# Ordering a two-block transformer program by a time-line simulation

## The chip, the core and the metric

The kernel runs on one core of a Trainium2 chip, in one launch. The metric is the device time of that core in microseconds (us). Its engines are TensorE (PE, with its weight loads as PEld), VectorE (DVE), ScalarE (ACT), GpSimd (POOL) and SyncE (SP), whose queue issues nearly all DMA transfers here. Each engine runs its own list of instructions in order and waits on semaphores for the others.

## What is computed

One sequence of 512 tokens of width 1024, in fp32, passes through three layers. The first is an RWKV-7 time mix with a squared-ReLU MLP. The second shares keys and values, runs a forgetting attention and a second MLP. The third adds two branches, a gated delta rule that runs forwards and backwards and a latent attention (MLA), and then an expert-choice mixture of 16 experts. The reference, cut to its frame:

```
def reference(x, c, ...):
    x = first_block(x, c, ...)      # for i in range(2): mix (rwkv7 | forgetting attention), then MLP
    return second_block(x, c_2, ...)

# second_block
h = rms_norm_2(x, g_mix) * (1.0 + sc1) + sh1
proj = h @ w_in
y_dn = gated_deltanet_branch(dn_qkv, dn_z, dn_b, dn_a, ...) @ w_o_dn
y_mla = mla_branch(c_q, c_kv, k_r, ...) @ w_o_mla
x = x + gt1 * ((g_dn * y_dn + g_mla * y_mla) @ w_out)
h = rms_norm_2(x, g_ffn) * (1.0 + sc2) + sh2
x = x + gt2 * expert_choice_ffn(h, w_router, w_gate, w_up, w_down)
return rms_norm_2(x, g_final)
```

Each of the three layers is modulated by shifts, scales and gates, which are products of a vector c with matrices of 1024 x 6144.

## The kernel before

Activations lie feature-major in SBUF, as eight tiles of 128 x 512 (128 features, 512 tokens). A dense product splits both operands into a high half in fp32r and a low half, and adds three products (lines 244 to 246 in dense_cols; 272 to 274 in dense_tmc; line 1323 in dense_gen). The split of weights is in wsplit: SP loads a raw tile (line 179), ACT copies it into the high half (line 181), and DVE or POOL subtracts to get the low half (line 183). Raw, high and low tiles have two buffers each. The split of activations is the same in two steps (lines 201 and 202).

The program is traced in one go and in the order of the layers, and the order of each engine's instructions is set afterwards, when the TileContext is left. The scheduler then runs a simulation of the chip; on each engine it issues, among the instructions whose inputs are ready at that simulated moment, the one with the best priority. The priority is the place in the trace, and "behind(by)" moves what is traced inside it back by so many places, so that it fills gaps. "issue_after(ins)" and "keep_in_program_order" add edges: what they cover is queued on its engine behind a given instruction, without a wait. Slots of a pool are given out in the same simulation. The order that comes out is fixed: at run time every engine takes its list as it stands.

The stages, with their times in the profiled execution: vectors of modulation and the dense products of the time mix (0 to 225 us), pairs and scan of the time mix (225 to 600), the first MLP (600 to 900), the forgetting attention (900 to 1275), the second MLP (1275 to 1575), the mixer with the delta rule (1575 to 2250), the rest of the latent attention and the output products (to 2470), the route and the 16 experts (to the end).

In the MLPs the modulation of the later layers is computed by DVE as a filler (mod_vgen, lines 376 and 378). In the mixer the delta rule's two head groups (dn_group) have normal priority, and the latent attention with the remaining input products (mla_gen, by way of dense_gen) is traced under behind(), a million places back, as the filler:

```
with self.behind():
    self.run(self.mla_gen(cks, H, ym))
self.run(self.dn_group(bp, lambda: tA, 0, gs, Zs, yd))
self.run(self.dn_group(bp, lambda: [self.fetch(t) for t in tB], 1, gs, Zs, yd))
```

Each group inverts 32 triangular blocks at once on DVE (tri_inverse2): 62 steps, each a multiply and an add (lines 1400 and 1402, then 1407 and 1409), then eight transposes (lines 1413 and 1414), behind which PE's small products start (line 1422). In the latent attention DVE multiplies by a gain and a norm (line 1812), and the result is split by lines 201 and 202.

The experts' weights come through a ring of 16 tiles of 1 MB (load, line 2081); the first five are queued between the loads of w_out by edges. Two experts share PE, 64 rows each (lines 2134 and 2162).

## Time and profile before

| what | value |
|---|---|
| median of 3 runs | 2994.79 us (2993.59 to 2998.83) |
| the profiled execution, its own time | 2999.24 us |
| its span, first to last instruction | 2997.4 us |
| PE busy, share of the span | 2766.3 us, 92% |
| DVE, ACT, POOL busy | 54%, 35%, 24% |
| mean granted clock of PE | 0.954 |

A page of the profile gives busy times by engine, a course in 40 slices and the costliest groups of instructions. The trace behind it is asked for tables by stretch of time, for who waited for whom, for the chain of work that ended last, and for the instructions of an engine in order of time. A wait is counted where an engine sat idle ahead of an instruction, and is put down to what ended it.

### The profile page before, as it was taken

How to read it: one execution, taken by the hardware profiler on the slowest of the kernel's cores; microseconds unless marked ns; L12 is line 12 of the kernel's file. 1: busy time of each engine (PE TensorE's matmuls, PEld its weight loads, DVE VectorE, ACT ScalarE, POOL GpSimd, SP SyncE). 2: the span in 40 equal slices, each digit the busy share in tenths (PEclk: the TensorE clock that was granted, in tenths of full speed). 3: DMA queues.
4: the chain of work that ended last, by engine and by line, in shares of the span. 5: the costliest groups of instructions: out<-in, count | busy, mean ns of one | idle time of the engine just before them, and what ended most of it. 6: DMA issues, size and time to landing. Idle time of an engine off the chain costs nothing. (4 is left out here: it accounts for less than half of the span.)

```text
span 2997.4 us, 38061 instructions
## 1 busy us (share of the span) xinstructions
PE 2766.3 (92%) x15046; PEld 1971.0 (66%) x15046; DVE 1615.5 (54%) x2449; ACT 1049.1 (35%) x1703; POOL 726.7 (24%) x563
## 2 busy tenths in 40 slices
PE   6998888999999999999999997998799997999997
PEld 1765666788876777788886775766677874444333
DVE  4568745465673367566636789638755442111112
ACT  2555523422234466422223542353344322110001
POOL 2456633211110043111113353144141121000000
PEclk9998777999999999999999999999999998999999
DMA  6324215355672321465432223142252359999998
GB/s 214 120 85 151 77 58 176 99 175 190 196 242 66 101 61 50 133 205 182 156 97 84 80 81 113 51 134 74 61 179 85 106 192 355 350 389 409 409 409 304
DMA packets 361010, 502.05 MB, mean 167 GB/s; under 512 B 24768, under 2 KB 236992, under 8 KB 360832
## 3 DMA queue, kind: packets, MB, share of 16 engines
q1 hardware_dynamic: 349600, 479.01, 47.0%
q10 hardware_dynamic: 11232, 20.62, 1.9%
q8 instruction: 118, 1.93, 0.3%
q14 instruction: 60, 0.49, 0.0%
HBM read 471.26 MB, written 26.21 MB: 166 GB/s over the span
## 5 line engine op out<-in xcount | busy, mean ns | idle before, releaser
L244 PE MATMUL psb<-s,wh 128*128 128x512 f32 x1384 | 542.8, 392 | 2.7 <-DVE s L988 1.9
L245 PE MATMUL psb<-s,wl 128*128 128x512 f32 x1384 | 540.4, 390 | 0.0
L246 PE MATMUL psb<-s,wh 128*128 128x512 f32 (+1 forms) x1320 | 514.7, 390 | 1.5 <-POOL s L481 0.6
L181 ACT ACTIVATE wh<-wr 128x1024 fp32r<-128x1024 f32 (+1 forms) x221 | 288.1, 1304 | 397.9 <-PE psb L246 263.9
L183 DVE TENSOR_TENSOR wl<-wr,wh 128x1024 fp32r<-128x1024 f32 (+1 forms) x145 | 260.7, 1799 | 262.8 <-ACT wh L181 260.4
L244 PEld LDWEIGHTS psb<-s,wh 128*128 128x128 f32 x1384 | 259.4, 187 | 70.7 <-issue 11.4
L245 PEld LDWEIGHTS psb<-s,wl 128*128 128x128 f32 x1384 | 259.5, 188 | 56.5 <-issue 2.2
L246 PEld LDWEIGHTS psb<-s,wh 128*128 128x128 f32 (+1 forms) x1320 | 247.4, 187 | 58.5 <-issue 2.9
L183 POOL TENSOR_TENSOR wl<-wr,wh 128x1024 fp32r<-128x1024 f32 (+1 forms) x76 | 185.5, 2443 | 401.4 <-ACT wh L181 386.1
L2134 PE MATMUL psb<-rg,s 128*64 128x512 f32 x1024 | 242.9, 597 | 5.7 <-DMA rg<-in_w_up_dram 4.4
L1323 PE MATMUL psf<-f,wh 128*128 128x512 f32 (+1 forms) x688 | 232.3, 412 | 10.7 <-ACT wh L181 10.7
L1019 POOL TENSOR_TENSOR s<-s 128x512 f32<-128x512 f32 x64 | 102.2, 1596 | 514.8 <-ACT s L1017 434.1
L2134 PEld LDWEIGHTS psb<-rg,s 128*64 128x64 f32 x1024 | 83.1, 136 | 142.6 <-issue 120.4
L1323 PEld LDWEIGHTS psf<-f,wh 128*128 128x128 f32 (+1 forms) x688 | 133.3, 195 | 42.5 <-ACT wh L181 11.6
L1323 PE MATMUL psf<-f,wl 128*128 128x512 f32 (+1 forms) x344 | 142.7, 415 | 16.6 <-POOL wl L183 16.5
L2162 PE MATMUL psb<-rg,s 128*64 128x512 f32 (+1 forms) x544 | 129.5, 620 | 0.0
L378 DVE SCALAR_TENSOR_TENSOR mt<-mr,crep,mt 128x512 f32<-128x512 f32 x168 | 126.4, 753 | 3.6
L201 ACT ACTIVATE s<-s 128x512 fp32r<-128x512 f32 x112 | 69.8, 625 | 136.2 <-POOL s L1019 73.1
L1026 DVE SCALAR_TENSOR_TENSOR s<-psb,aff,s 128x512 f32<-128x512 f32 x64 | 45.9, 751 | 129.1 <-PE psb L246 129.1
L1323 PE MATMUL psb<-f,wh 128*128 128x512 f32 (+1 forms) x336 | 106.5, 397 | 7.8 <-DVE f L479 5.9
L1017 ACT ACTIVATE s<-psb 128x512 f32<-128x512 f32 x64 | 37.6, 588 | 164.0 <-PE psb L246 164.0
L2162 PEld LDWEIGHTS psb<-rg,s 128*64 128x64 f32 x544 | 46.2, 147 | 73.9 <-issue 69.8
(565 smaller groups left out, 4926.4 us busy)
## 6 DMA issues: line engine op xcount, KB each, us to landing
rg<-in_w_gate_dram SPq DMA_DIRECT2D x64, 1024.0 KB
rg<-in_w_up_dram SPq DMA_DIRECT2D x64, 1024.0 KB
rg<-in_w_down_dram SPq DMA_DIRECT2D x64, 1024.0 KB
mr<-in_mod_w_dram SPq DMA_DIRECT2D x96, 512.0 KB
wr<-in_mlp_down_dram SPq DMA_DIRECT2D x32, 1024.0 KB
wr<-in_mlp_up_dram SPq DMA_DIRECT2D x31, 1024.0 KB
wr<-in_w_in_dram SPq DMA_DIRECT2D x54, 512.0 KB
mr<-in_w_mod_dram SPq DMA_DIRECT2D x40, 512.0 KB
```

Source lines behind the costliest of these rows:

```text
L181: nc.scalar.activation(hi, raw, AF.Copy)
L183: (lo_eng or self.lo_eng or nc.vector).tensor_tensor(lo, raw, hi.bitcast(F32), op=OP.subtract)
L201: nc.scalar.activation(hi, src, AF.Copy)
L244: nc.tensor.matmul(pt[:mw], hi[k][:, j:j + mw], a, start=(k == 0), stop=False)
L245: nc.tensor.matmul(pt[:mw], lo[k][:, j:j + mw], a, start=False, stop=False)
L246: nc.tensor.matmul(pt[:mw], hi[k][:, j:j + mw], b, start=False, stop=(k == nk - 1))
L378: nc.vector.scalar_tensor_tensor(acc[:, hb], raw[:, d], c, acc[:, hb], op0=OP.mult, op1=OP.add)
L1019: nc.gpsimd.tensor_tensor(sq, r, r, op=OP.mult)
L1026: nc.vector.scalar_tensor_tensor(xT[m], pt, gt[:, m:m + 1], xT[m], op0=OP.mult, op1=OP.add)
L1323: nc.tensor.matmul(pt[:rows, :cols], x, y, start=(k == 0 and q == 0), stop=(k == nk - 1 and q == 2))
L2134: nc.tensor.matmul(B[n][q], XE[hp][k0 // 2][:, o:o + 64], w[e][:, k, n * 512:n * 512 + 512], start=(k0 + k == 0), stop=(k0 + k == 7), skip ...
L2162: last = nc.tensor.matmul(pt[q, :n], HT[(k + i) // 4][:, o:o + 64], w[e][i], start=(k + i == 0), stop=(k + i == 7), skip_group_check=True)
```

## The change

The context that traces and orders the program is opened with one more argument. By it the scheduler picks instructions along another simulation: one that plays the time line of each engine with its sequencer and its queues, and of the DMA queues, in place of the coarser simulation that is the default. The traced program, its priorities, edges, pools and tiles are the same.

```
--- before.py
+++ after.py
@@ -2426,7 +2426,7 @@
         A[n] = nc.dram_tensor(nm, a.shape, mybir.dt.from_np(a.dtype), kind="ExternalInput").ap()
         feed[nm] = a
     out = nc.dram_tensor("out_0_dram", (D, T), F32, kind="ExternalOutput").ap()
-    with _tile.TileContext(nc) as tc:
+    with _tile.TileContext(nc, schedule_with_timeline_sim=True) as tc:
         K(tc, nc, A, coff, poff).program(out)
     nc.finalize()
     r = _run(nc, [feed], core_ids=[0])
```

## Rows read from the trace of the kernel before

**Rows 1.** The page's first part: busy us, share of the span and count by engine.

```profile
PE 2766.3 (92%) x15046; PEld 1971.0 (66%) x15046; DVE 1615.5 (54%) x2449; ACT 1049.1 (35%) x1703; POOL 726.7 (24%) x563
```

**Rows 2.** Busy us by stage; last three columns: granted clock, DMA share, GB/s.

```profile
225.00:600.00 375.00, 325.51 (x2858) 242.09 (x2855) 242.16 (x322) 159.33 (x265) 165.64 (x193) 0.82 0.34 112
600.00:900.00 300.00, 297.49 (x1340) 241.29 (x1339) 191.46 (x221) 83.62 (x85) 41.03 (x26) 1.00 0.62 201
900.00:1275.00 375.00, 364.92 (x1781) 273.58 (x1781) 196.13 (x431) 203.33 (x376) 87.36 (x56) 1.00 0.28 82
1275.00:1575.00 300.00, 300.00 (x1341) 244.53 (x1340) 167.25 (x174) 85.26 (x88) 48.72 (x31) 1.00 0.49 159
1575.00:2250.00 675.00, 589.89 (x3667) 467.15 (x3665) 475.84 (x787) 266.21 (x477) 242.43 (x130) 0.95 0.32 95
2250.00:2425.00 175.00, 173.59 (x911) 137.28 (x910) 94.08 (x157) 69.77 (x134) 34.22 (x26) 1.00 0.32 103
2700.00:2997.00 297.00, 269.88 (x1170) 114.27 (x1166) 55.60 (x91) 28.62 (x47) 0.00 (x0) 0.97 0.97 383
```

**Rows 3.** The chain that ended last (start, us, what); one slice of the tail.

```profile
2811.20 20.40 DMA rg<-in_w_up_dram
...
2775.00:2850.00 75.00, 70.55 (x314) 29.92 (x312) 10.45 (x17) 5.83 (x10) 0.00 (x0) 0.98 1.03 409
```

**Rows 4.** Waits of PE in the whole span: us in total, times, longest us.

```profile
PE psb L1422 <- DVE T L1413: 27.2, 6, 13.2
...
PE psf L1323 <- POOL wl L183: 16.5, 11, 2.1
...
PE psf L1323 <- ACT wh L181: 10.7, 1, 10.7
PE psb L828 <- ACT W L824: 9.8, 5, 6.8
```

**Rows 5.** PE in order of time at the two inverses; in brackets the idle time before.

```profile
1877.43 0.28 PE L1422 MATMUL psb<-T,UB 32*32 32x32 f32 x2 [10.26 <-DVE T L1413]
...
2117.72 0.28 PE L1422 MATMUL psb<-T,UB 32*32 32x32 f32 x2 [13.18 <-DVE T L1413]
...
2118.53 0.63 PE L1323 MATMUL psf<-f,wl 128*128 128x512 f32 x1
...
2119.81 0.63 PE L1323 MATMUL psf<-f,wl 128*128 128x512 f32 x1
```

**Rows 6.** DVE and POOL in order of time in the two inverses.

```profile
1787.43 1.79 DVE L1400 TENSOR_TENSOR tm<-P,R 128x135 f32<-128x135 f32 x1
...
1872.00 2.28 DVE L1409 TENSOR_TENSOR R<-R,tm 128x87 f32<-128x87 f32 x1
...
2047.24 2.31 DVE L1402 TENSOR_TENSOR R<-R,tm 128x60 f32<-128x60 f32 x1
...
2055.45 2.55 POOL L183 TENSOR_TENSOR wl<-wr,wh 128x1024 fp32r<-128x1024 f32 x1 [5.99 <-ACT wh L181]
...
2055.78 2.47 DVE L1402 TENSOR_TENSOR R<-R,tm 128x231 f32<-128x231 f32 x1
2058.29 0.41 DVE L1400 TENSOR_TENSOR tm<-P,R 128x240 f32<-128x240 f32 x1
...
2102.22 2.57 DVE L1407 TENSOR_TENSOR tm<-P,R 128x255 f32<-128x255 f32 x1
```

**Rows 7.** ACT and DVE in order of time around 2066 us.

```profile
2066.66 0.63 ACT L201 ACTIVATE g<-f 128x512 fp32r<-128x512 f32 x1 [10.77 <-DVE f L1812]
...
2073.16 1.04 ACT L181 ACTIVATE wh<-wr 128x1024 fp32r<-128x1024 f32 x1
...
2065.89 0.74 DVE L1812 SCALAR_TENSOR_TENSOR f<-f,P,f 128x512 f32<-128x512 f32 x1
```

**Rows 8.** A group of instructions by line: busy us, mean ns, idle before.

```profile
L183 POOL TENSOR_TENSOR wl<-wr,wh 128x1024 fp32r<-128x1024 f32 (+1 forms) x76 | 185.5, 2443 | 401.4 <-ACT wh L181 386.1 <-PE psb L281 7.4 <-PE psf L1323 5.6
```

**Rows 9.** Waits of SP's queue of DMA issues: us in total, times, longest.

```profile
SPq L179 <- POOL wl L183: 572.6, 74, 29.1
```

More of the change, by code (lines that the diff above doesn't have):

```diff
@@ L2428 @@
     out = nc.dram_tensor("out_0_dram", (D, T), F32, kind="ExternalOutput").ap()
-    with _tile.TileContext(nc) as tc:
+    with _tile.TileContext(nc, schedule_with_timeline_sim=True) as tc:
         K(tc, nc, A, coff, poff).program(out)
```

## The prediction

> **What bounds the kernel now.** I read the page's first line, then the table by stage, then the waits of TensorE, then the time lines around its longest waits. TensorE (PE) is busy for 2766.3 of 2997.4 us, so it has 231 us of idle time in all [rows 1]. The table by stage says where that is [rows 2]. In three stretches that hold 775 us (600 to 900, 1275 to 1575, 2250 to 2425) PE is busy for 297.49, 300.00 and 173.59 us: 3.9 us of idle time at the full clock. There the order can lose time, but it has almost none to win. In the last stretch the DMA share is 0.97, and the chain of waits goes through transfers of the expert weights of 20.4 us at a time [rows 2, 3]: what orders the engines changes nothing there, except by when the ring of weights starts to fill. Two stretches are left in which order matters both ways: the scan of the first block (225 to 600, 49.5 us of idle time at a clock of 0.82) and the delta rule with latent attention as its filler (1575 to 2250, 675 - 589.89 = 85.1 us of idle time at 0.95) [rows 2].
>
> In the second of these the waits have names. PE waits 27.2 us for DVE's transposes of the triangular inverse, 16.5 us for POOL's low halves of filler weights and 10.7 us for ACT's high half of one [rows 4]. The two longest waits at the inverse are 13.18 and 10.26 us, and what PE runs right behind each are filler matmuls (line 1323) [rows 5]: PE works in order, and the order has the inverse's first two matmuls ahead of filler.
>
> **The change part by part.** No instruction is added to the trace and none is taken out, beyond the waits and table loads that follow from the order. What changes is the clock by which the scheduler picks: on each engine it takes the ready instruction of the best priority at a simulated moment. Priorities (the arguments of "behind"), the edges of issue_after and keep_in_program_order, slots and banks stay. So every wait is kept or moved by which of two ready instructions goes first, on PE, DVE, ACT and POOL and on SP's queue of DMA issues alike.
>
> First, are today's waits errors of the old order's clock? For the inverse I compared its steps. A step of 128x231 takes 2.47 us and the next, of 240, takes 0.41; the long one starts at 2055.78, while POOL's split of 1024 columns runs from 2055.45 for 2.55 us [rows 6]. Such long steps stand 13 times in the first group's inverse (from 1787.43 to 1872.00) and 8 times in the second's (2047.24 to 2102.22) [rows 6], each 1.1 to 2.3 us over its neighbours; at 2 us in the mean that is 26 and 16 us, against waits of PE of 10.3 and 13.2 us. So the stretching alone is more than the wait. An order that prices every instruction by itself keeps these 23.4 us; one that prices the collision, or that had DVE too short before, wins them. I take 0, the first of the two, as the rows explain the wait without an error of price; the end for the range is -23.4 us.
>
> The Trainium skill, "SBUF — State Buffer", section "Who interferes with whom", says that a DVE instruction with two SBUF inputs and a GpSimd instruction that reads SBUF exclude each other for the whole instruction. The trace agrees (2.47 against 0.41 us), and by this rule no price of single instructions tells when the inverse ends.
>
> The wait of 10.7 us is another kind. ACT stands for 10.77 us at a split (line 201) for a multiply of DVE (line 1812), and the high half of filler weights (line 181), which PE needs, is queued behind it at 2073.16; DVE runs these multiplies one by one between steps of the inverse [rows 7]. That is an order on ACT that took DVE's multiply for earlier than it came. Better times of DVE turn it: -10.7 us, bounds 0 and -10.7. I take all of it. The 16.5 us for POOL are the filler's own supply (2443 ns a split [rows 8]); with the inverse unfinished PE has nothing else, so 0 here, -16.5 at best.
>
> What does a new order cost where PE is full? The trace has no other order, so I bound it. The nearest rows are stretches in which the same dense code runs beside chains: 900 to 1275 has 10.1 us of idle time in 375 (2.7%), 1575 to 2250 has 85.1 in 675 (12.6%) [rows 2]. At 2.7% the 775 full us lose 20.9, or 17 more than now; at 12.6% they lose 98, or 94 more; where the new order agrees with the old, nothing. I take 17, as dense stretches with double-buffered weights are nearer to attention than to the inverse; ends 0 and 94. Behind a long wait three matmuls take 1.28 us (2118.53 to 2119.81 [rows 5]), 427 ns each, where 1341 of them fill 300 us at the full granted clock, 224 ns each [rows 2]: the lower of PE's two levels against the upper; some eight run so before the clock is back, 1.6 us for each such wait. For three new ones I add 5 us.
>
> In the two stretches with chains every pick is a new draw. Of the 85.1 us, 27.2 + 16.5 + 10.7 = 54.4 are named above, which leaves 30.7 us; of the scan's 49.5 us the largest group is 9.8 us in five waits, the longest of them 6.8 us [rows 2, 4]. These are hand-offs in small pieces, which an order from other times would undo as well as mend. I take a seventh of the 80 us as lost, 12 us, since chains that lie well can move only one way; ends -24 and +40 (30% won, half lost).
>
> SP's queue of issues is the fifth list that is ordered anew. It stands 572.6 us before weight loads (line 179) until POOL has freed a buffer [rows 9], so it runs as far ahead as the buffers let it. An issue that goes ahead of another one costs if the passed one is the next that is needed, and all loads queued behind it wait too; I take 0, with the longest single wait of this group, 29.1 us, as the end.
>
> The tail is the experts. The first loads of their ring go out between the loads of w_out, by explicit edges, and those edges stay, so 0; if the first five loads came after all of them, five loads of 1 MB at 409 GB/s [rows 3] would be 13 us, one for one at the end.
>
> Sum against the profiled execution of 2999.24 us: -10.7 + 17 + 5 + 12 = +23, so 3022.5. That execution stood 4.4 us above the median of 2994.79, so the forecast is 3018 us.
>
> **The rivals.** *The new times are the better ones, and the order wins.* For it: the 10.77 us on ACT are a mistake of timing, and the inverse has a stall in both groups. Against it: the stalls are explained by the collisions, and 775 us are full. It gives the 10.7, the 9.8, half of the 23.4 and of the 16.5 us, and a quarter of the other 70 us: 58 us, with 5 us of clock 63, less 22 us for waits and clock in the full stretches: 41 us, so some 2954 us. It decides if the new clock has DVE and POOL within some per cent of the trace (0.41 and 2.4 us); ends 2915 and 2989. Chance 0.38.
>
> *More collisions.* POOL's splits come earlier or later and meet more two-input steps of DVE. Each costs 2.06 us; less than a third of POOL's 76 splits of weights [rows 8] lie in the inverses. If 30 more meet a DVE chain that sets the pace, 62 us on DVE, of which PE cannot fill half: 31 us beside the 23 of the forecast, some 3050 us; it decides from about ten new meetings on. Chance 0.10.
>
> *The order hardly moves,* because edges and program order fix it, or the flag changes only times and no pick: 2989 to 3001 us, within 0.2%, about what a measurement of this kernel can tell from no change. Against it: the fillers are placed by readiness alone. Chance 0.12.
>
> **How the numbers follow.** Forecast (slower by new waits in full stretches and chains): 3018 us, 0.40, its own range 3001 to 3090. The collisions add 0.10 on the same side. Faster by over 0.2% 0.38, within 0.2% 0.12, slower by over 0.2% 0.50. The range of 8 in 10 goes from 2940, which leaves out the far end of the faster case, to 3090, near the bound of 94 us.
>
> **What would show it.** Right: in the table by stage PE falls under 297 of 300 us in 600 to 900 or 1275 to 1575, with new waits of PE for a low or high half of weights (lines 181 and 183); the waits of line 1422 for line 1413 stay above 15 us; the last stretch keeps its DMA share and its length from the first expert matmul to the end. The ACT wait for line 1812 should be gone. Wrong: the inverse's wait vanishes and the filler runs ahead of it (the first rival), or the idle time by stage is as it was and the difference lies in the tail, by a ring that starts to fill sooner or later. A kernel above 3100 us would mean that a queue was ordered badly as a whole, for example SP's issues, which I have priced at 29.1 and 13 us at most.

## The result and the profile after

The new order takes 3068.85 us (median of 4 runs, 3060.34 to 3070.32), the old one beside it 2996.20 us (4 runs): a ratio of 1.0239, 95% interval 1.0224 to 1.0254, so 72.7 us slower. The forecast was 3018 us, in a range of 2940 to 3090. The direction and the range held; the size did not, and the place of the loss was another one.

The page's first line answers [rows 1]. The work is the same, and PE is busy 27.4 us longer for the same 15046 matmuls (2793.7 against 2766.3), in a span that is 71.1 us longer:

```profile
span 3068.5 us, 38050 instructions
...
PE 2793.7 (91%) x15046; PEld 2000.8 (65%) x15046; DVE 1600.0 (52%) x2449; ACT 1051.6 (34%) x1706; POOL 733.3 (24%) x563
```

Next the table by stretch of time, with the columns of [rows 2], in the new kernel: the scan, a stretch of each MLP, the tail, and one slice of the tail.

```profile
225.00:600.00 375.00, 328.75 (x2877) 247.42 (x2876) 253.52 (x332) 163.44 (x273) 176.33 (x202) 0.82 0.34 111
600.00:900.00 300.00, 300.00 (x1358) 244.46 (x1357) 195.37 (x226) 84.25 (x86) 43.64 (x27) 1.00 0.63 203
1350.00:1650.00 300.00, 300.00 (x1347) 245.58 (x1346) 163.87 (x170) 82.90 (x83) 43.03 (x27) 1.00 0.47 148
2770.00:3068.00 298.00, 269.63 (x1170) 114.23 (x1166) 55.48 (x91) 28.63 (x47) 0.00 (x0) 0.98 0.98 383
2850.00:2925.00 75.00, 70.51 (x307) 29.64 (x305) 10.45 (x17) 5.83 (x10) 0.00 (x0) 0.98 1.03 409
```

The MLPs are as full as before (300.00 of 300, against 297.49 and 300.00), the scan is nearly as it was (328.75 against 325.51 us busy, clock 0.82 in both), and the tail has its 409 GB/s and its length. So the time must be lost between. Fixed stretches of time compare different work once a kernel is late, so the next table cuts both traces at the same instruction: the last update of the first MLP and that of the second (line 1026), and w_out's last matmul (line 246). First the two stretches of the kernel before, then those of the new one.

```profile
904.80:1613.40 708.60, 698.51 (x3269) 545.96 (x3268) 380.65 (x622) 297.69 (x473) 142.45 (x91) 1.00 0.37 113
...
1613.40:2469.05 855.65, 768.75 (x4599) 608.43 (x4597) 567.82 (x942) 339.10 (x616) 275.63 (x156) 0.96 0.35 105
```

```profile
906.90:1663.40 756.50, 722.67 (x3269) 562.54 (x3268) 379.40 (x622) 296.87 (x473) 148.62 (x91) 0.97 0.35 106
...
1663.40:2538.20 874.80, 768.78 (x4604) 618.01 (x4602) 547.84 (x943) 342.31 (x618) 272.92 (x156) 0.93 0.34 103
```

This is the account of the loss. The attention with the second MLP takes 47.9 us more (756.50 - 708.60): 24.2 us because the same 3269 matmuls are busy longer (722.67 - 698.51, at a lower clock), and 23.7 us of idle time (33.83 - 10.09). The mixer and the output products take 19.2 us more (874.80 - 855.65), all of it idle time, as PE's busy time is the same to 0.03 us. What lies ahead of 904.80 adds 2.1 us, what lies behind 2469.05 adds 1.9 (530.3 - 528.4). The sum is 71.1 us, the difference of the spans.

The waits of PE in the whole span, with the columns of [rows 4]:

```profile
PE psb L1422 <- DVE T L1413: 55.1, 6, 28.3
...
PE psb L828 <- ACT W L824: 13.0, 3, 7.0
...
PE psb L1224 <- DVE s L1221: 8.7, 8, 3.2
PE psb L1194 <- ACT qk L1172: 8.6, 6, 3.9
...
PE psf L1890 <- ACT f L1898: 6.6, 1, 6.6
PE psb L1657 <- POOL s L1651: 6.5, 1, 6.5
```

In the mixer the waits for weight halves are nearly gone: from 1600 to 2480 the matmuls of line 1323 that write tile psf wait 2.4 us for POOL and 0.2 for ACT, against 16.5 and 10.7 in [rows 4] (those that write psb wait 4.4 us for halves, 3.0 more than before). But the inverses' wait has doubled, from 27.2 to 55.1 us. In the attention there are more and longer waits, of 1 to 4 us (lines 1224 and 1194). Slices of the attention in the new kernel show what goes with them:

```profile
1050.00:1075.00 25.00, 25.00 (x99) 16.96 (x98) 1.23 (x1) 8.00 (x12) 5.58 (x3) 1.00 0.29 84
1075.00:1100.00 25.00, 17.07 (x74) 13.41 (x73) 13.84 (x36) 15.96 (x32) 14.40 (x9) 0.86 0.25 66
...
1125.00:1150.00 25.00, 22.37 (x101) 16.78 (x100) 12.33 (x39) 12.11 (x29) 7.76 (x5) 0.77 0.10 26
```

From 1125 to 1150 PE is busy for 22.37 of 25 us, but the granted clock is 0.77. In the old kernel these slices hold 24.3 to 24.6 us of work at 1.00.

The share of busy time hides how the clock fell, because matmuls at the lower clock are themselves busy for longer. Here is the same stretch, cut where the clock changes (columns of [rows 2]), and the waits of PE ahead of the fall (columns of [rows 5]):

```profile
1119.00:1123.70 4.70, 1.69 (x11) 1.25 (x12) 3.34 (x7) 4.58 (x13) 4.35 (x4) 0.92 0.41 99
1123.70:1133.20 9.50, 9.47 (x33) 6.84 (x34) 4.93 (x21) 2.95 (x9) 0.00 (x0) 0.50 0.13 38
1133.20:1142.00 8.80, 8.26 (x42) 6.12 (x41) 3.04 (x8) 2.04 (x5) 0.89 (x1) 1.00 0.01 2
...
1119.99 0.38 PE L1194 MATMUL psb<-qk,qk 68*128 68x256 f32 x1 [1.07 <-ACT qk L1172]
1121.43 1.31 PE L1224 MATMUL psb<-s,V 128*64 128x128 f32 x10 [1.06 <-ACT s L1219]
1123.73 0.45 PE L1216 MATMUL psb<-C,s 128*128 128x128 f32 x1 [0.99 <-DVE st L1202]
```

PE first stands idle for 3.0 of 4.7 us, in three waits of about 1 us, two of them for ACT. Behind them it runs the small matmuls of the chain for 9.5 us almost without a gap, but at 0.50, the lower of its two levels. It is back at 1.00 when the next block of filler runs.

What stands behind it is seen on ACT, in order of time, where a pair of heads begins: first the new kernel, then the old. Lines 1171 to 1173 are the copies that prepare q and k of a head, line 1201 is the exponential of a unit (its sums of 0.19 us are left out), line 1219 copies transposed scores.

```profile
1116.71 0.61 ACT L1171 ACTIVATE qk<-s 64x512 fp32r<-64x512 f32 x1
1117.35 0.63 ACT L1173 ACTIVATE qk<-s 64x512 fp32r<-64x512 f32 x1
1118.00 0.63 ACT L1171 ACTIVATE qk<-s 64x512 fp32r<-64x512 f32 x1
1118.65 0.63 ACT L1173 ACTIVATE qk<-s 64x512 fp32r<-64x512 f32 x1
1119.31 1.28 ACT L1172 ACTIVATE qk<-s 64x512 fp32r<-64x512 f32 x2
1120.61 0.40 ACT L1201 ACTIVATE s<-s,st 128x128 f32<-128x128 f32 x1
```

```profile
1112.55 0.63 ACT L1172 ACTIVATE qk<-s 64x512 fp32r<-64x512 f32 x1
1113.09 0.39 ACT L1201 ACTIVATE s<-s,st 128x128 f32<-128x128 f32 x1
...
1113.59 0.63 ACT L1171 ACTIVATE qk<-s 64x512 fp32r<-64x512 f32 x1
1114.17 0.39 ACT L1219 ACTIVATE s<-psb 128x256 f32<-128x256 f32 x1
1114.58 0.51 ACT L1201 ACTIVATE s<-s,st 128x256 f32<-128x256 f32 x1
...
1115.21 0.63 ACT L1172 ACTIVATE qk<-s 64x512 fp32r<-64x512 f32 x1
1115.86 0.62 ACT L1201 ACTIVATE s<-s,st 128x384 f32<-128x384 f32 x1
```

The new list runs the copies of both heads of a pair as one block of 3.9 us (1116.71 to 1120.6) ahead of four exponentials, and does so in each of the eight pairs. In the old list the second head's copies stand one by one between exponentials. The two waits of PE for ACT shown above fall into this block and just behind it. PE's new list fits this: the scores of the next three units stand with their second matmuls put off, transposes stand right ahead of the products that need their copies, and the gate's filler comes in blocks of 19 and 7 per eight units. That is read from the two lists of instructions; what each costs, the experiments tell as far as they can.

### The profile page after: what moved, and what is told of

Read it like the earlier page. It is cut to its first block, busy times and chain, and to the rows that moved or that the text cites. A ratio compares the mean times of both kernels' runs of the same rounds, so it can differ in the third digit from the quotient of the medians.

```text
span 3068.5 us, 38050 instructions
## 1 busy us (share of the span) xinstructions
PE 2793.7 (91%) x15046; PEld 2000.8 (65%) x15046; DVE 1600.0 (52%) x2449; ACT 1051.6 (34%) x1706; POOL 733.3 (24%) x563
## 4 chain that ended last, share of the span: by engine, by line
PE 76%; DVE 12%; DMA 7%; ACT 3%; issue 2%; POOL 0%; SPq 0%; DVEq 0%; ACTq 0%; POOLq 0%
PE psb L244 11%; PE psb L246 11%; PE psb L245 11%; PE psf L1323 6%; PE psb L2134 6%; PE psb L1323 4%; PE psb L2162 3%; DMA rg<-in_w_down_dram 2%; PE psb L1224 2%; DMA rg<-in_w_gate_dram 1%; DMA rg<-in_w_up_dram 1%; PE psm L342 1%; PE psb L273 1%; PE psb L274 1%; PE psb L272 1%
## 5 line engine op out<-in xcount | busy, mean ns | idle before, releaser
L1323 PE MATMUL psf<-f,wh 128*128 128x512 f32 (+1 forms) x688 | 222.5, 400 | 0.2 <-ACT wh L181 0.2
```

The lines of the kernel that those rows point to most:

```text
L1323: nc.tensor.matmul(pt[:rows, :cols], x, y, start=(k == 0 and q == 0), stop=(k == nk - 1 and q == 2))
```

## The experiments

Most of them hold lists. All instructions have the same names in both kernels, so a list of one order can be put on the other kernel by edges without waits. In these kernels lines of the code stand 2 further down (line 1224 is 1226), with edges in the mixer up to 9 further.

```
+def _order(tc, nc):
+    ins = {i.name: i for i in nc.cur_bb.bb.instructions}
+    for part in zlib.decompress(base64.b85decode(_LISTS)).decode().split(";"):
+        names = [f"I-{n}" for n in itertools.accumulate(int(d) for d in part.split(":")[1].split(","))]
+        for a, b in zip(names, names[1:]):
+            tc.add_manual_dep(ins[b], a, mybir.DependencyInfo(mybir.DependencyClass.NoSync, mybir.DependencyReason.DATA), reason="order")
...
         K(tc, nc, A, coff, poff).program(out)
+        _order(tc, nc)
```

**Which stage loses.** The kernel before, with the new order of all five engines in one part alone.

> The kernel before, with the new order of all five engines for the instructions of the forgetting attention alone. By the landmarks of the two traces the last update of the first MLP (line 1026) comes 2.1 us later (904.8 to 906.9) and that of the second 50.0 us later (1613.4 to 1663.4), so if each stage's loss is its own this kernel is 48 us slower than before, with a granted clock near 0.8 to 0.95 between 1075 and 1250. If the loss comes of the prediction's full stretches or of the mixer, or if it needs the new order of the stages around it, it is within 10 us of before.

> The kernel before, with the new order for the mixer and its output products alone (from the projections of the delta rule to w_out). By the landmarks the shift grows from 50.0 us to 69.2 us there (last matmul of w_out 2469.05 to 2538.2), so +19 us if stages add up: PE loses the waits for the halves of filler weights (16.5 and 10.7 us), and waits some 28 us more at line 1422. If the mixer's loss in the new kernel is only that of a stage that starts 50 us later against transfers, it is within 5 us of before.

> The kernel before, with the new order for the time mix alone. Landmarks: the first square of the first MLP (line 1019) moves from 557.2 to 563.4, so +6 us if it stays; the prediction had put half of its loss of 12 us in scan and mixer here. If the first MLP makes it up (its last update moves by 2.1 us only), +2.

> The kernel before, with the new order for the two MLPs and for the route and the experts. The prediction's step of new idle time in full stretches would give +17 to +22 us. By the landmarks: -4 us in the first MLP (its start is late by 6.2 us, its end by 2.1), +1.5 in the route and experts, so between -4 and +2.

| new order in | us | before, same chip | difference, us | ratio, 95% |
|---|---|---|---|---|
| attention | 3052.48 | 2996.05 | +56.4 | 1.0172 to 1.0203 |
| mixer, output products | 3010.23 | 2996.05 | +14.2 | 1.0036 to 1.0061 |
| time mix | 2995.23 | 2996.05 | -0.8 | 0.9992 to 1.0010 |
| MLPs, route, experts | 2992.98 | 2996.05 | -3.1 | 0.9977 to 0.9995 |

The parts add up to 66.7 of the 72.7 us. The attention holds three quarters of the loss, the mixer most of the rest; the MLPs lose nothing, against the 17 to 22 us of the forecast.

**The attention put back.** The new kernel, with the old lists of the attention.

> The new kernel with the old order of all five engines in the forgetting attention alone. If the stages are independent, the 56 us come back: 3068.9 - 56 = 3013 us, 14 to 18 us slower than before, which is the mixer. If the new order elsewhere needs the new attention, less comes back.

3021.22 against 2998.32 us before on that chip (ratio 1.0075, 1.0059 to 1.0091): 22.9 us are left of 72.7, so 50 came back. That is 5 to 9 us less than expected, near what the landmarks gave (47.9).

**PE's list or ACT's.** In the attention of the kernel before: PE's new list beside the four old ones; and ACT's new list with the other four chosen around it by the old scheduler.

> The kernel before; in the forgetting attention PE's list is that of the new kernel, the lists of ACT, DVE, POOL and SP are its own. If the loss of 56 us lies in PE's order (gate matmuls taken in one block of 19 to 24 ahead of the chain, scores pulled ahead of transposes), this kernel is 40 to 56 us slower than before. If it lies in ACT's order (the six copies of two heads in one block ahead of the exponentials), PE's order alone costs under 20 us.

> The kernel before; in the forgetting attention ACT's list is that of the new kernel (six copies of lines 1171 to 1173 in one block before the exponentials of line 1201), the other four lists are chosen anew around it by the old scheduler. If ACT's block is the cause: 30 to 56 us slower than before, as each block holds the exponentials up for 3.9 us in each of eight pairs of heads, with the clock behind it. If PE's order is the cause: under 15 us.

PE's list alone: 3039.01 against 2995.02 us, +44.0 (ratio 1.0135 to 1.0165). ACT's: 3068.48, +73.5 (1.0231 to 1.0262), more than all five new lists together. Both theories claimed 30 to 56 us for themselves and under 20 for the other, so neither expectation came true. PE's list does most of the damage by itself, and the other four new lists together add 12.4 us to it (56.4 - 44.0). The second kernel is no price of ACT's list alone, as there the old scheduler also changed the other four lists; it shows that this scheduler, held to ACT's block, finds an order worse than the new one. The waits of PE in the attention of that kernel show how ACT's block reaches PE (line 1226 is the product with V, line 1221 ACT's copy of transposed scores, which stands behind the block):

```profile
PE psb L1226 <- ACT s L1221: 31.2, 7, 5.7
PE psb L1226 <- DVE s L1223: 5.7, 2, 3.5
PE psb L1196 <- ACT qk L1174: 4.3, 1, 4.3
```

**The block broken in two,** in the new kernel.

```
-            nc.scalar.activation(a[lo], tq[q], AF.Copy)
-            nc.scalar.activation(c[lo], tk[q], AF.Copy)
-            nc.scalar.activation(b[up], tq[q], AF.Copy)
+            with tc.issue_after(self.last_act()) if hd else contextlib.nullcontext():
+                nc.scalar.activation(a[lo], tq[q], AF.Copy)
+                nc.scalar.activation(c[lo], tk[q], AF.Copy)
+                nc.scalar.activation(b[up], tq[q], AF.Copy)
```

> The new kernel with one edge: the three ACT copies of the odd head are queued behind the last ACT instruction traced before them, so that the block of six falls apart into two blocks of three. If ACT's block is the cause, 30 us or more of the 56 come back (about 3035 us or less). If PE's order is the cause, it stays within 15 us of the new kernel (3055 to 3075 us).

3056.65 us, ratio 1.0203 (1.0186 to 1.0220) against 1.0239 of the new kernel: 11 us came back. Two blocks of three copies cost less than one of six, but far from all is ACT's: the 11 us are near the 12.4 us that the lists besides PE's add.

**PE's list taken apart.** The old kernel with a PE list made of both: the chain in the new order with the gate's 206 filler matmuls at their old places, and the reverse.

> The kernel before; in the forgetting attention only PE's list is changed, and in it only the order of the chain (scores, transposes, products with V) is the new one, with the 206 gate matmuls left at their old places between the units. PE's whole new list cost 44 us. If the chain's order is the cause (in each eight units the second score matmuls of three units stand together behind products, and transposes stand right ahead of the products that need their copies), 30 to 44 us slower than before. If the filler's place is the cause, under 12.

> The counterpart: PE's chain in its old order, the 206 gate matmuls at their new places (blocks of 19 and 7 per eight units, none in the second half). If the filler taken ahead in blocks is the cause, 30 to 44 us slower than before; if the chain's order is, under 12.

The chain's order costs 16.2 us (3014.52 against 2998.32), the filler's places 22.8 us (3021.10); together 39.0 of the 44.0. Here too both expectations wanted one cause, and there are two of like size. The stretch 1069 to 1260 (columns of [rows 2]) tells them apart: new chain, new filler, PE's whole new list, all five new lists.

```profile
1069.00:1260.00 191.00, 182.08 (x984) 137.11 (x984) 118.69 (x344) 116.61 (x255) 61.20 (x41) 1.00 0.27 78
```

```profile
1069.00:1260.00 191.00, 170.63 (x913) 130.15 (x912) 117.42 (x339) 110.30 (x249) 56.88 (x39) 0.95 0.25 74
```

```profile
1069.00:1260.00 191.00, 166.61 (x883) 125.78 (x882) 111.51 (x331) 104.90 (x239) 56.05 (x39) 0.95 0.21 60
```

```profile
1069.00:1260.00 191.00, 162.79 (x805) 122.68 (x804) 103.35 (x325) 101.34 (x235) 57.16 (x37) 0.86 0.19 52
```

With filler between the units the clock stays at 1.00 even if the chain is badly ordered (182.08 of 191 us busy; the kernel before has 183.51 there). With filler in blocks, half of the units run with nothing between them, PE waits for DVE's copies (12.3 us in ten waits at line 1226), and the clock is 0.95; with the other four lists, ACT's block among them, it is 0.86.

**Filler held back in the mixer.** In the old order 447 of 1584 filler matmuls (line 1323) stand ahead of the last matmul before the first inverse and 1084 before the second; in the new one 758 and all 1584, and the latent attention too. Two edges on PE hold filler until the chain's matmul.

```
+        held = [self.fill_mm[k] for k in (447, 1084)]
...
+        for ins, last in zip(held, self.inv_after):
+            self.tc.add_manual_dep(ins, last.name, mybir.DependencyInfo(mybir.DependencyClass.NoSync, mybir.DependencyReason.DATA), reason="issue_after")
```

> The new kernel with two edges on PE in the mixer: filler matmul 447 of 1584 is queued behind the last matmul ahead of the first inverse, and filler matmul 1084 behind the last one ahead of the second, as many as the old order had put there (the new one has 758 and all 1584). If the mixer loses because the filler is used up before the second group's chain, the 14 us come back and the waits saved for halves of weights stay saved: 14 to 40 us faster than the new kernel (3028 to 3055 us), with the wait of 28 us at line 1422 under 15. If the filler's place is not the cause, within 5 us of it.

3079.34 us, ratio 1.0280 (1.0265 to 1.0295): 12 us slower than the new kernel. The count was off: 312 of the 1584 matmuls are traced earlier and are not in this list, so the edges stood at 759 and 1396, and the first held nothing. The next kernel has them at 135 and 772, on top of the old attention.

> The same with two edges on PE in the mixer, at other places than in the kernel with the two edges above, where the first edge changed nothing: filler matmul 135 of mla_gen's 1272 behind the last matmul ahead of the first inverse and number 772 behind the last one ahead of the second, so that the filler stands 519 and 1156 matmuls far at these points (old order 447 and 1084, new order 758 and 1584). If the filler that overtakes the chain is the mixer's cause, 14 us or more come back, to 3000 us or less; with the waits for weight halves saved as well, some 2985. If it is not, it is within 5 us of the kernel without the edges, or slower.

3034.42 us, 13 us slower than without the edges (3021.22). Filler held back in this way gives nothing back. The inverses' wait went down from 55.1 to 11.3 us, as the theory said, but the idle time came up elsewhere: waits of PE from 1600 to 2450, where line 1553 is the chain ahead of the inverse and lines 1325, 1405 and 1788 are lines 1323, 1400 and 1779 of the kernel before.

```profile
PE psb L1553 <- ACT s L1550: 14.3, 16, 1.2
PE psf L1325 <- DVE f L1788: 13.7, 1, 13.7
PE psf L1325 <- DVE tm L1405: 12.4, 1, 12.4
PE psb L1427 <- DVE T L1418: 11.3, 6, 3.8
```

The 12.4 us stand at the first edge (before 1808.17), the 13.7 us inside the second inverse (before 2168.94), where the filler that is next needs DVE. Cut at the inverses, PE's idle time from the last update of the second MLP to w_out's last matmul is 104.7 us with the edges and 104.8 without them. Behind the second inverse it went from 33.3 to 7.1 us, ahead of the two inverses from 27.9 to 64.0. The 12.3 us that this stretch became longer are busy time (783.6 against 771.2 us for 4608 matmuls each): the clock from the first inverse to the second is 0.88, without the edges 0.95.

**Filler put where the wait is.** The kernel before, with the first matmuls behind the inverses queued behind more filler: 46 and 107, or 46 and 54.

```
+        self.inv_fill = [self.fill_mm[k] for k in (527, 1107)]
...
+        filled = self.inv_fill.pop(0)
...
+                self.tc.add_manual_dep(i1.ins, filled.name, mybir.DependencyInfo(mybir.DependencyClass.NoSync, mybir.DependencyReason.DATA), reason="issue_after")
```

> The kernel before with two edges on PE: the first matmuls behind the inverses (line 1422) are queued behind filler matmul 527 and 1107 of mla_gen's 1272, that is 46 and 107 more filler matmuls than in the old order, 10 and 24 us of work at 224 ns each, in the waits of 10.3 and 13.2 us and the one of 10.7 us for ACT. If PE's filler sets the mixer's time, 15 to 30 us faster than before (2965 to 2980 us). If the chain's own length sets it, or the filler's weights don't come faster (POOL's halves), within 5 us, and the waits at line 1323 grow by what those at line 1422 lose.

> The same with 54 instead of 107 more filler matmuls ahead of the second inverse's first matmul (12 us for its wait of 13.2 us alone). If filler sets the time: 10 to 22 us faster than before; more than with 107 only if those overshoot the inverse's end and hold the chain up.

3004.98 us with 107 (ratio 1.0027, 1.0018 to 1.0037) and 3001.09 with 54 (1.0013, 1.0004 to 1.0022), against 2997.09: slower, where filler as the limit wanted 10 to 30 us faster. The waits of PE with 107, in the whole span, name a reason:

```profile
PE psf L1323 <- DVE f L1785: 27.0, 1, 27.0
...
PE psf L1323 <- POOL wl L183: 19.1, 12, 2.2
...
PE psb L1425 <- DVE T L1416: 8.7, 3, 3.5
```

The wait did not go, it changed its name: the filler that is next needs a multiply of the rotary embedding on DVE (line 1779 of the kernel before, 1785 here). DVE comes to it at 2138.51, behind the last steps of the inverse, its eight transposes (2117.08 to 2131.97) and the tables of the embedding; the chain's first matmul, held behind this filler, starts at 2150.85. So 107 are too many, and the filler that is next in the list is not free of DVE; whether later filler could go ahead of it was not tried. With 54 the waits at line 1425 are 28.4 us in seven pieces, no less than the 27.2 us before: in the old order PE ran nine or ten filler matmuls in each gap between the transposes, and the edges took these out, so that behind a first wait of 9.8 us three more of 3.4 us each stand open. These two kernels move cover more than they add it.

**A kernel that beats both.** The first of these with the new order of the parts that were not slower, and these parts alone.

> The first of these two with the new order of the time mix, both MLPs, route and experts, which alone were 1 and 3 us faster than before. If the parts add up, 4 us faster than the kernel with the two edges alone.

> The kernel before with the new order for the time mix, both MLPs, route and experts; attention, mixer and output products keep the old one. If the parts are independent, -0.8 and -3.1 us add up to 4 us faster than before (about 2993 us). If the time mix's gain is noise, 3 us; if the new order only helps beside the new attention, no difference.

3001.22 us, 3.8 faster than without these parts, but still behind the old kernel (1.0007 to 1.0025); and 2996.69 against 2997.40 alone (0.9986 to 1.0005), no difference. The MLPs, route and experts had shown -3.1 us by themselves; the time mix with them shows -0.7. No kernel here beats the old one by more than these 3 us, which did not come again.

## Why the prediction was right and wrong

**The step that failed is the first one of the sum: which stretches count.** The prediction split the span in full ones (775 us), the tail, and "two stretches in which order matters both ways". The attention, 900 to 1275, was in none of them. It came in only as a yardstick for others, with its 10.1 us of idle time in 375 [rows 2], and had no term of its own. It is the third chain: 64 units, each through PE, DVE, ACT and PE again, with a filler of 206 matmuls. That it was 97% full did not mean that order matters little there, but that its order was good; it lost 56.4 us by the run that changed it alone, 47.9 by the landmarks (with the MLP behind it), and 50 came back when its old order was restored. With the forecast's own way of pricing it could have had 10.1 us at the full clock turned into the mixer's 12.6% of idle time: 375 x 0.126 = 47 us, less 10, is 37. The bound was in the rows.

**New waits in the full stretches, +17, and their clock, +5: not there.** 300.00 of 300 us in both MLPs, and -3.1 us in the run. The granted clock there is 1.00, as before. Why the dense code keeps its pace under either scheduler was not tried. The yardstick was the wrong way round: what was lost, the attention lost.

**Scan and mixer, +12, and the wait for ACT, -10.7: together +1.3, measured 13.4** (-0.8 and +14.2 us). That the 12 alone is near is luck: the scan lost nothing, and the mixer's waits did not add up as the sum had them. The wait for ACT went as forecast (0.2 us now), and so did 14.1 of the 16.5 us for POOL that the forecast had put at 0. But in the mixer and the output products the idle time grew by 19.1 us all the same. Cut at the inverses (from the first step to the first matmul of line 1422), PE is idle for 49.5 us beside the two inverses before and 43.7 now; ahead of them it is 24.5 and 28.0. What is lost lies behind the second inverse, 12.9 us before and 34.3 now, in a shorter stretch:

```profile
2117.70:2469.05 351.35, 338.46 (x2136) 270.74 (x2136) 192.55 (x304) 138.22 (x260) 85.11 (x56) 0.99 0.40 127
...
2312.60:2538.20 225.60, 191.30 (x1318) 160.35 (x1318) 109.26 (x158) 62.34 (x109) 24.84 (x20) 0.89 0.39 130
```

The first line is the kernel before, which still has filler to run there; the second is the new one, in which the last of the 1584 filler matmuls ran at 2156, 89 us ahead of the second inverse.

**The inverses' wait, 0: the price was wrong, and so was its reason.** The prediction put the wait down to DVE steps that POOL stretches. In the second inverse of the new order (2245.66 to 2310.36) one of the 124 steps is stretched, to 1.41 us, and the others are not, as POOL has almost nothing left to do there; and PE waits longer than ever. These are that inverse's steps of the forms of [rows 6], and PE behind it, in order of time:

```profile
2258.64 1.41 DVE L1402 TENSOR_TENSOR R<-R,tm 128x231 f32<-128x231 f32 x1
2261.25 0.39 DVE L1400 TENSOR_TENSOR tm<-P,R 128x240 f32<-128x240 f32 x1
...
2312.64 0.31 PE L1422 MATMUL psb<-T,UB 32*32 32x32 f32 x2 [28.27 <-DVE T L1413]
```

The Trainium skill, "SBUF — State Buffer", section "Who interferes with whom", says that such a DVE instruction and a GpSimd instruction exclude each other; this trace agrees (POOL is busy 2.83 of the 50 us from 2250, and the one step of 1.41 us stands beside POOL's split of 1.29 us from 2258.51), but the wait does not follow from it. The wait of 28.3 us follows from what PE has beside the second inverse: nothing, as the filler was used up (1584 of 1584 matmuls ahead of the second group's first). Of the 27.9 us by which the waits at line 1422 grew, 15.1 are this, 3.7 the wait behind the first inverse (10.26 to 13.99, with filler left), and the rest mostly three waits of 3.4 us between the transposes of the second. In every order tried PE waits for DVE somewhere: filled with more filler the wait turns into one of 27.0 us for DVE, held back it moves ahead of the inverses and into the second. So the mixer's 14 us are idle time that the new order gathers behind the second inverse; by which few picks, no run here settles, and the cause of these 14 us stays open.

**The queue of SP, 0 with an end of 29.1.** SP stands 123.8 us once, at a fetch (line 1266) into a slot that the second group's chain frees late (line 1582). It was a wait beyond the bound; what it costs by itself was not tried, so this term stays open. **The tail, 0:** 1.9 us, right.

**The rivals.** "More collisions" is refuted: 11 long steps in the first inverse and one in the second, against 13 and 8 [rows 6], and yet slower. "Hardly moves" too. "The order wins" was right on two of the four waits that it named, those for weight halves (10.7 and 16.5 us); the wait of 9.8 us at line 828 is now 13.0, and the inverses' has doubled. It was wrong that the first two are worth anything at the end: 24.6 us of them went, and the mixer became slower.

## What to carry to other kernels

The stretch that was full beside a chain of small steps is the one that the new order spoilt most here: price such a stretch by what a like chain loses where it lies badly, not by the idle time that it has. When a scheduler is exchanged, hold the lists stage by stage and engine by engine: the loss then has an address, and a wait that vanishes can be told from a wait that only moved. A filler has an order of its own to keep: in the orders tried here more of it at a wait gained nothing, because it came out of another gap or needed the engine that the chain was waiting for.

## What the hardware showed that was not expected

A busy share of nine tenths can hide a stall and what it costs. The slice of 22.37 of 25 us at 0.77 (1125 to 1150) looks like a PE that is throttled while it works. Cut finer, the fall stands behind 4.7 us of which PE was busy for 1.69, and the lower level then held for 9.5 us in which PE was busy throughout, until a block of filler ran. The same chain in the same bad order, with filler spread between the units, kept 1.00 at 182.08 of 191 us. Of the 47.9 us that the attention and the MLP behind it lost, 24.2 are busy time, which no list of waits shows: in the pair of heads cut here, three waits of about 1 us were followed by 9.5 us at the lower level.
